# Two-layer diffusion backbone with top-2-of-8 experts: weights of the small experts split by halves, another order of products, and weighting, spreading and gather in other chunks

## Chip, cores and metric

One core of one Trainium2 chip runs the whole kernel in one launch. The metric is device time in microseconds (us), the median of several runs. The compute engines are named as in the profile: PE is the matrix engine (PEld its weight loads), DVE the vector engine, ACT the scalar engine, POOL the GpSimd engine, and SP issues the DMA transfers. Each engine works its instructions off in program order.

## The reference, cut to what matters

The layer stack is a short gated convolution with a dense feed-forward block (layer 0) and differential attention with a mixture of experts (layer 1). The change lies in the mixture of experts alone:

```python
def moe_ffn(a, w_r, b_r, w1, w3, w2):          # a: 256 tokens x 1024
    logits = (a @ w_r).astype(jnp.float32) + b_r.astype(jnp.float32)
    top_v, top_i = lax.top_k(logits, TOP_K)    # 2 of 8 experts for each token
    gates = jax.nn.softmax(top_v, axis=-1)
    ...
    # for each expert, on its tokens xs:
    #   (silu(xs @ w1) * (xs @ w3)) @ w2, times the gate, added back at the token
```

The feed-forward width is 2816, so an expert has 34.6 MB of weights in float32, and all eight together 277 MB.

## The kernel before, in words

**Two parts.** float32 values are split in two parts in a fast matrix format (F32R): a first part (`hi`, by a cast on ACT, L88) and the rest (`lo`, by a subtraction on DVE, L92). A product of split weights and split activations takes three matmuls (`mm3`, L200 to L202). The output stays close to a float32 product.

**Units.** Weights come in units of 128x2048 float32 (1 MB). `Loads` issues one DMA for each unit, in the order in which units are used, as soon as one of the raw slots (`rw`, `ra`, `rp`, `rq`) is free. `Parts` turns raw units into `hi`, `lo` in one of three slots: `Parts.unit()` gives the next unit to the caller, and before that it frees the slot of the unit used before and calls `pump`, which puts the cast and the subtraction of the next unit that isn't split yet into the queues of ACT and DVE. So the splits stand in the program where units are taken, about two units ahead of their use. `engines(u)` says in how many pieces a unit is split: two halves of 1024 columns for the units of the large experts, one piece of 2048 for those of the small experts.

**Experts.** The experts 2 to 7 are put in an order by their counts on the chip (`choose`). Places 2, 4 and 6 (`FEW`) hold at most 64 tokens, the others at most 128. For a small expert the two parts of its 64 tokens stand side by side as 128 columns, so a product needs two matmuls, by `hi` and by `lo` of the weights (`two`, L1237). Some units of the small experts (`whole`, the second unit of chunks 1, 4, 7 and 10) aren't split at all: they are used raw, with plain float32 matmuls (L1234).

**Chunks.** The hidden width is cut in 11 chunks. The main loop goes over the 88 pairs of expert and chunk, `g`. A chunk `c` of expert `e` does in this order: it takes its first unit and multiplies (`up`, first half of the 1024 inputs); it takes the unit of w2 of chunk `g-2` and multiplies (`finish`, `down`, into `y`); it turns the hidden values of chunk `g-1` (`hidden`: PE, then ACT and DVE in turn); it takes its second unit and multiplies (`up`, second half), and ACT copies or activates the result (`act`).

**Work between the experts.** Once the last `down` of an expert is done (two chunks into the next expert) `weighted` scales `y` by the gates and splits it (two ACT, two DVE instructions, from the one buffer of `y`), after the second of the four products of the second `up`. `spread` brings the result back to the tokens: eight matmuls in two PSUM tiles of the tag `g` (`psg`, two buffers) and four DVE instructions (L1308) that add to the stream. It is called twice, at the end of chunks 2 and 3. In an odd expert `gather` fetches the tokens of the next two experts in eight steps at the end of chunks 2 to 9: each step has four matmuls into a `psg` tile, an ACT or DVE instruction, two casts and, one step later, two subtractions. At the end a second loop over the experts serves only counts above the capacity; the trace has nothing of it.

Of the kernel before, what the change touches and what calls it, by code (L numbers as in the profile page):

```python
# [11 lines left out]
F32 = mybir.dt.float32  # L12
# [8 lines left out]
P = 128  # L21
D = 1024
KT = D // P
T = 256
T2 = 2 * T
# [11 lines left out]
FEW = (2, 4, 6)  # L37
# [105 lines left out]
def backbone(ctx: ExitStack, tc: tile.TileContext, i, out):  # L143
    nc = tc.nc
    V, A, PE, PO = nc.vector, nc.scalar, nc.tensor, nc.gpsimd
# [15 lines left out]
    units = [i["w0"][u] for u in range(49)] + [i["w1"][u] for u in range(16)]  # L161
    chosen, chunks = [], [(e, c) for e in range(NE) for c in range(NCH)]

    def moe_unit(e, u):

        if e < 2:
            return i["moe"][e, u]
        return lambda: i["moe"][bass.ds(chosen[e - 2], 1), u].rearrange("a p c -> (a p) c")


    whole, uses = [], []
    for g, (e, c) in enumerate(chunks):
        uses.append((e, 3 * c))
        if g > 1:
            uses.append((chunks[g - 2][0], 3 * chunks[g - 2][1] + 2))
        if e in FEW and c % 3 == 1:
            whole.append(len(units) + len(uses))
        uses.append((e, 3 * c + 1))
    uses += [(NE - 1, 3 * c + 2) for c in (NCH - 2, NCH - 1)]
    few = {len(units) + k for k, (e, _) in enumerate(uses) if e in FEW}  # L180
    units += [moe_unit(*u) for u in uses]
    ada_slots = raw_slots(const, 2, "ra")
    raws = raw_slots(const, 3, "rw")
# [3 lines left out]

    def engines(u):

        if u >= 69 and u not in few:  # L190
            return [(c, [(V, c)]) for c in (slice(0, 1024), slice(1024, U))]
        return [(ALL, [(V, ALL)])]

# [5 lines left out]
    def mm3(ps, wh, wl, xh, xl, first, last):  # L199
        PE.matmul(ps, wh, xh, start=first, stop=False)  # L200
        PE.matmul(ps, wh, xl, start=False, stop=False)  # L201
        PE.matmul(ps, wl, xh, start=False, stop=last)  # L202
# [149 lines left out]
    start = ExitStack()  # L352
# [8 lines left out]
    ps = [psc.tile([P, T2], F32, name=f"cb{n}") for n in range(4)]  # L361
# [48 lines left out]
    c = [sums(0)]  # L410
# [12 lines left out]
    run = ada_pe(1)  # L423
# [10 lines left out]
    def bank():  # L434
        return psp.tile([P, T2], F32, name="mm")
# [6 lines left out]
    w = parts  # L442
    first = [bank() for _ in range(6)]
# [16 lines left out]
    run = ada_pe(3)  # L460
# [30 lines left out]
    with tc.tile_pool(name="sc", bufs=1, reuse_waits="tile") as pc:  # L491
# [23 lines left out]
        for j in range(2, KT):  # L515
            ps = [bank() for _ in range(3)]
# [6 lines left out]
        ps = [bank() for _ in range(4)]  # L523
# [51 lines left out]
    with tc.tile_pool(name="ac", bufs=1, reuse_waits="tile") as pc, tc.tile_pool(name="ffn", bufs=9, reuse_waits="tile") as hp:  # L575
# [7 lines left out]
        def h_tile():  # L583
            return hp.tile([P, T2], F32R, name="hh"), hp.tile([P, T2], F32R, name="hl")
# [9 lines left out]
        h = [h_tile() for f in range(2)]  # L594
        ws = [[next(w) for k in range(2 * KT)] for f in range(2)]
        for s in range(2):
            for f in range(2):
                ps = [bank()[:, :T] for _ in range(2)]
# [8 lines left out]
        for gi, n in enumerate(GROUPS):  # L607
            while len(h) < n:
                ps = [bank() for _ in range(2)]
# [15 lines left out]
            for m in range(4 if lastg else KT):  # L625
                f = bank()
# [5 lines left out]
            h = []  # L632
# [64 lines left out]
    first = project(0, bank)  # L697
# [530 lines left out]
        V.tensor_copy(gs, ps)  # L1228
        return back, gs

    def two(ps, x, w, c, first, last):

        if w[1] is None:
            PE.matmul(ps, x.bitcast(F32), w[0][:, c], start=first, stop=last)  # L1234
        else:
            for b in range(2):
                PE.matmul(ps, x, w[b][:, c], start=first and b == 0, stop=last and b == 1)  # L1237

    def up(ps, xs, h, w, ks=range(4)):
        for k in ks:  # L1240
            c = slice(k * T2, (k + 1) * T2)
            a = h == k == 0, h == 1 and k == 3
            if len(xs) == 3:
                two(ps, xs[2][:, 4 * h + k], w, c, *a)
            else:
                mm3(ps, xs[0][:, 4 * h + k], xs[1][:, 4 * h + k], w[0][:, c], w[1][:, c], *a)

    def act(ps, few=False):
        if few:
# [8 lines left out]
    def hidden(g, few=False):  # L1258
        pt = pst.tile([P, T], F32, name="ht")
        if few:  # L1260
            for f in range(4):
                PE.matmul(pt[:, f * H:(f + 1) * H], g[:, f * P:(f + 1) * P], fold, start=True, stop=True)
            g = px.tile([P, P], F32, name="hg")
            A.activation(g, pt[:, :P], AF.Silu)
            V.tensor_tensor(out=g, in0=pt[:, P:], in1=g, op=OP.mult)
            hb = px.tile([P, T], F32R, name="hh").rearrange("p (f b s) -> p f b s", f=2, b=2)
            g = g.rearrange("p (f s) -> p f s", f=2)
            A.copy(hb[:, :, 0], g)
            V.tensor_tensor(out=hb[:, :, 1], in0=g, in1=hb[:, :, 0].bitcast(F32), op=OP.subtract)
            return [hb]  # L1270
        for f in range(2):
            PE.transpose(pt[:, f * P:(f + 1) * P], g[:, f * P:(f + 1) * P], ident)
        hh = px.tile([P, T], F32R, name="hh")
        hl = px.tile([P, T], F32R, name="hl")
        A.copy(hh, pt)  # L1275
        V.tensor_tensor(out=hl, in0=pt, in1=hh.bitcast(F32), op=OP.subtract)
        return hh, hl

    def down(y, h, w, first, last):
        for f, n in ((0, 0), (1, 0), (0, 1), (1, 1)):  # L1280
            b = slice(f * P, (f + 1) * P)
            c = slice(f * D + n * T2, f * D + (n + 1) * T2)
            a = first and f == 0, last and f == 1
            if len(h) == 1:
                two(y[n], h[0][:, f].rearrange("p b s -> p (b s)"), w, c, *a)
            else:
                mm3(y[n], h[0][:, b], h[1][:, b], w[0][:, c], w[1][:, c], *a)

    def weighted(y, g):

        yh, yl = ([px.tile([P, T2], F32R, name=f"{a}{n}") for n in range(2)] for a in ("yh", "yl"))
        for n in range(2):
            A.activation(yh[n], y[n], AF.Identity, scale=g)
        for n in range(2):
            V.scalar_tensor_tensor(yl[n], y[n], g, yh[n].bitcast(F32), op0=OP.mult, op1=OP.subtract)
        return list(zip(yh, yl))

    def spread(n, w, back):

        for k in range(4 * n, 4 * n + 4, 2):  # L1300
            ps = psg.tile([P, 2, T], F32, name="g")
            for j in range(2):
                c = slice((k + j) % 4 * P, ((k + j) % 4 + 1) * P)
                for b in range(2):
                    PE.matmul(ps[:, j], w[b][:, c], back, start=b == 0, stop=b == 1)
            for j in range(2):
                x = X[0][k + j]
                V.scalar_tensor_tensor(x, ps[:, j], mod1[20 + k // 2][:, j, 0:1], x, op0=OP.mult, op1=OP.add)  # L1308
# [14 lines left out]
    run, got, rets = gather(), {}, {}  # L1323
# [3 lines left out]
    res, parted, acts, hids, y = None, deque(), {}, {}, None  # L1327
# [10 lines left out]
    for g, (e, c) in enumerate(chunks):  # L1338
        n, pr, few_now = e % 2, e // 2, e in FEW
        ps = psh.tile([P, T2], F32, name="h13")  # L1340
        w = parts.unit()
        for k in range(4):
            if g == 0:
                next(run)
            up(ps, got[pr][n], 0, w, [k])
        if g == 0:
            next(run)
            for _ in range(2):
                parts.give(1)
            parts.holding = False  # L1350
        if g > 1:
            y = finish(g - 2)
            if chunks[g - 2][1] == NCH - 1:
                e0 = chunks[g - 2][0]
                res = y, rets[e0 // 2][1][:, e0 % 2:e0 % 2 + 1], rets[e0 // 2][0][:, e0 % 2]
        if g > 0:
            hids[g - 1] = hidden(acts.pop(g - 1), chunks[g - 1][0] in FEW)
        if g == 1:
            gates()
        if g == 2:  # L1360
            places_of()
            V.tensor_tensor(out=fold, in0=ident[:, :H], in1=ident[:, H:], op=OP.add)
        if g == 4:
            choose()
        w = parts.unit()
        for k in range(4):
            up(ps, got[pr][n], 1, w, [k])
            if k == 1 and res is not None:
                parted.extend((m, v, res[2]) for m, v in enumerate(weighted(*res[:2])))
                res = None  # L1370
        acts[g] = act(ps, few_now)
        if parted and c > 1:
            spread(*parted.popleft())
        if n == 0 and c == 4:
            rets[pr] = returns(pr)
        if n == 1 and e < NE - 1:
            if c == 1:
                for t in range(2):
                    onehot(t, pr + 1)
                run = gather(pr + 1)  # L1380
            if 2 <= c < 2 + KT:
                got[pr + 1] = next(run)
    y = finish(g - 1)
    hids[g] = hidden(acts.pop(g))
    y = finish(g)
    for n, w in enumerate(weighted(y, rets[3][1][:, 1:2])):
# [4 lines left out]
    _, count = nc.values_load_multi_w_load_instructions(r["cnti"][:1], min_val=0, max_val=T,  # L1391
                                                        skip_runtime_bounds_check_because="counts of 256 tokens")
    with tc.If(count[0] > 0):
        for e in range(NE):
            with tc.If(count[1 + e] > 0):
                n = e % 2
# [6 lines left out]
                y = acc()  # L1403
                for c in range(NCH):
                    w = []
# [7 lines left out]
                    ps = psh.tile([P, T2], F32, name="h13")  # L1413
# [88 lines left out]
```

## Time and profile before

| | us |
|---|---|
| median of 3 runs | 1651.02 (1650.89 to 1652.36) |
| the profiled execution | 1652.38 |
| its span, first to last instruction | 1650.7 |
| mixture of experts, first `up` to the end | 822.7 to 1650.7 |

The busy shares over the whole span are PE 94%, PEld 77%, DVE 78%, ACT 52%, POOL 3%; 400 MB come in by DMA at 243 GB/s on average. A matmul's record reaches to the end of its pipeline, so PE records overlap; the step from the start of one matmul to the next is what it costs. In a timeline a number in brackets is the time for which the engine sat idle ahead of the row, and what ended it.

### The profile page before, as it was taken

What the parts mean: (1) busy time and instruction counts of PE and PEld (TensorE: products, weight loads), DVE (VectorE), ACT (ScalarE), POOL (GpSimd) and SP (SyncE); (2) the same over time, 40 slices, a digit from 0 to 9 for tenths busy, and PEclk for the clock granted to TensorE, in tenths of its full rate; (3) what the DMA queues carried; (4) which work ended last, traced back from release to release, by engine and by line L of the source; (5) the groups of instructions that cost most, each with busy time, mean ns of one, the idle gap of its engine ahead of it and who ended that gap; (6) DMA issues with size and microseconds to landing.
All of it is one profiled execution on the core that took longest, in us unless ns stands there. A gap on an engine that the chain in (4) does not pass through costs nothing. (4 is left out here: it accounts for less than half of the span.)

```text
span 1650.7 us, 20590 instructions
## 1 busy us (share of the span) xinstructions
PE 1553.3 (94%) x7569; PEld 1264.6 (77%) x7569; DVE 1281.9 (78%) x1799; ACT 866.1 (52%) x1163; POOL 44.9 (3%) x162
## 2 busy tenths in 40 slices
PE   8799899999999999998899999888998889988997
PEld 7687688888888888887878778666786667866785
DVE  5888887668658666667588988878888788977896
ACT  3222244222212243445577768666676667866774
POOL 0000000000000002113000000000000000000000
PEclk9899999999999999999999999999999999999999
DMA  9345524445547424223469978889799997889990
GB/s 360 104 161 203 201 104 156 176 132 200 179 160 279 174 80 151 77 77 128 153 260 368 351 312 344 342 336 347 295 341 350 361 363 307 345 330 357 352 357 30
DMA packets 55727, 400.33 MB, mean 243 GB/s; under 512 B 6449, under 2 KB 6481, under 8 KB 7105
## 3 DMA queue, kind: packets, MB, share of 16 engines
q1 hardware_dynamic: 55298, 398.50, 64.4%
q8 instruction: 61, 1.00, 0.2%
q0 software_dynamic: 320, 0.44, 0.2%
q14 instruction: 48, 0.39, 0.1%
HBM read 397.87 MB, written 1.05 MB: 242 GB/s over the span
## 5 line engine op out<-in xcount | busy, mean ns | idle before, releaser
L92 DVE TENSOR_TENSOR wl<-rw,wh 128x1024 fp32r<-128x1024 f32 (+1 forms) x187 | 319.0, 1729 | 110.8 <-ACT wh L88 108.6
L88 ACT CAST wh<-rw 128x1024 fp32r<-128x1024 f32 (+1 forms) x186 | 264.8, 1453 | 63.3 <-PE mm L201 56.4
L200 PE MATMUL mm<-ah,wh 128*128 128x512 f32 (+1 forms) x576 | 221.5, 385 | 8.0 <-ACT ah L340 7.2
L202 PE MATMUL mm<-ah,wl 128*128 128x512 f32 (+1 forms) x576 | 221.1, 384 | 6.2 <-DVE wl L92 6.1
L201 PE MATMUL mm<-al,wh 128*128 128x512 f32 (+1 forms) x576 | 220.8, 383 | 0.0
L92 DVE TENSOR_TENSOR wl<-rp,wh 128x1024 fp32r<-128x1024 f32 (+1 forms) x122 | 174.9, 1465 | 35.0 <-ACT wh L88 31.4
L280 DVE SCALAR_TENSOR_TENSOR junk<-ra,cb 128x1024 bf16<-128x1024 f32 x136 | 166.3, 1223 | 3.3
L88 ACT CAST wh<-rp 128x1024 fp32r<-128x1024 f32 (+1 forms) x122 | 147.4, 1244 | 4.4 <-issue 1.7
L200 PE MATMUL h<-wh,xs 128*128 128x512 f32 x352 | 144.5, 410 | 0.0
L201 PE MATMUL h<-wl,xs 128*128 128x512 f32 x352 | 139.5, 396 | 0.0
L202 PE MATMUL h<-wh,xs 128*128 128x512 f32 x352 | 139.4, 396 | 0.0
L200 PEld LDWEIGHTS mm<-ah,wh 128*128 128x128 f32 x576 | 110.5, 192 | 30.2 <-ACT ah L340 8.5
L202 PEld LDWEIGHTS mm<-ah,wl 128*128 128x128 f32 x576 | 110.2, 191 | 28.9 <-DVE wl L92 8.4
L92 DVE TENSOR_TENSOR wl<-ra,wh 128x1024 fp32r<-128x1024 f32 (+1 forms) x81 | 114.5, 1444 | 20.2 <-ACT wh L88 19.4
L92 DVE TENSOR_TENSOR wl<-rq,wh 128x1024 fp32r<-128x1024 f32 (+1 forms) x87 | 124.3, 1476 | 6.8 <-ACT wh L88 6.4
L201 PEld LDWEIGHTS mm<-al,wh 128*128 128x128 f32 x576 | 110.3, 191 | 21.5 <-DVE al L335 0.9
L88 ACT CAST wh<-rq 128x1024 fp32r<-128x1024 f32 (+1 forms) x87 | 104.2, 1256 | 0.0
L88 ACT CAST wh<-ra 128x1024 fp32r<-128x1024 f32 (+1 forms) x81 | 96.7, 1230 | 2.7 <-PE h L202 2.0
L1237 PE MATMUL h<-wh,xl 128*128 128x512 f32 x216 | 89.9, 416 | 0.0
L1237 PE MATMUL h<-wl,xl 128*128 128x512 f32 x216 | 86.0, 398 | 2.3 <-DVE wl L92 2.3
L201 PE MATMUL y<-wl,hh 128*128 128x512 f32 x220 | 87.1, 396 | 1.1 <-DVE wl L92 1.1
L200 PE MATMUL y<-wh,hh 128*128 128x512 f32 x220 | 87.4, 397 | 0.5 <-ACT hh L1275 0.5
(328 smaller groups left out, 3057.1 us busy)
## 6 DMA issues: line engine op xcount, KB each, us to landing
rw<-moe SPq DMA_DIRECT2D x81, 1024.0 KB, 5.5
rp<-moe SPq DMA_DIRECT2D x77, 1024.0 KB, 5.7
rw<-w SPq DMA_DIRECT2D x61, 1024.0 KB, 4.9
rq<-moe SPq DMA_DIRECT2D x54, 1024.0 KB, 6.0
ra<-moe SPq DMA_DIRECT2D x52, 1024.0 KB, 5.7
ra<-ada SPq DMA_DIRECT2D x44, 1024.0 KB, 5.1
rx<-ada SPq DMA_DIRECT2D x4, 1024.0 KB, 19.7
rp<-w SPq DMA_DIRECT2D x4, 1024.0 KB, 6.6
```

The source lines that it names most:

```text
L88: self.nc.scalar.copy(hi[:, c0], raw[:, c0])
L92: engine.tensor_tensor(out=lo[:, c], in0=raw[:, c], in1=hi[:, c].bitcast(F32), op=OP.subtract)
L200: PE.matmul(ps, wh, xh, start=first, stop=False)
L201: PE.matmul(ps, wh, xl, start=False, stop=False)
L202: PE.matmul(ps, wl, xh, start=False, stop=last)
L280: V.scalar_tensor_tensor(junk, raw[:, a * D:(a + 1) * D], 1.0, cb[:, s], op0=OP.mult, op1=OP.mult, accum_out=m[:, a, s:s + 1])
L1237: PE.matmul(ps, x, w[b][:, c], start=first and b == 0, stop=last and b == 1)
```

## The change

The units of the small experts are split in two halves of 1024 columns, as those of the large experts are. The second unit of chunks 1, 3, 5, 7 and 9 is used whole, in place of 1, 4, 7 and 10. Products with first parts lead: for a small expert `few_up` issues two products with `hi` ahead of the two with `lo`, and `down` does the same for each half of its unit; for a large expert the product with the weights' `lo` comes third in place of second (`mm3w`), and `down` takes both outputs of the first half of its unit before the second half. In the loop `weighted` stands ahead of the second unit, and the first `spread` at the same place one chunk later, the second one at the end of that chunk: both are in chunk 2. `gather` runs in chunks 3 to 10. Other lines are as they were; the number of DMA transfers is the same.

```diff
-        if e in FEW and c % 3 == 1:
+        if e in FEW and c % 2:
             whole.append(len(units) + len(uses))
...
-        if u >= 69 and u not in few:
+        if u >= 69:
             return [(c, [(V, c)]) for c in (slice(0, 1024), slice(1024, U))]
         return [(ALL, [(V, ALL)])]
...
+    def few_up(ps, x, w, h, ks):
+
+        for b in range(2 if w[1] is not None else 1):
+            for k in ks:
+                v = x[:, 4 * h + k]
+                PE.matmul(ps, v.bitcast(F32) if w[1] is None else v, w[b][:, k * T2:(k + 1) * T2], start=h == k == b == 0,
+                          stop=h == 1 and k == 3 and (b == 1 or w[1] is None))
+
+    def mm3w(ps, xh, xl, wh, wl, first, last):
+        PE.matmul(ps, xh, wh, start=first, stop=False)
+        PE.matmul(ps, xl, wh, start=False, stop=False)
+        PE.matmul(ps, xh, wl, start=False, stop=last)
...
     def down(y, h, w, first, last):
-        for f, n in ((0, 0), (1, 0), (0, 1), (1, 1)):
...
+        for f in range(2):
+            cs = [slice(f * D + n * T2, f * D + (n + 1) * T2) for n in range(2)]
             if len(h) == 1:
-                two(y[n], h[0][:, f].rearrange("p b s -> p (b s)"), w, c, *a)
+                for b in range(2):
+                    for n in range(2):
+                        PE.matmul(y[n], h[0][:, f].rearrange("p b s -> p (b s)"), w[b][:, cs[n]], start=first and f == b == 0,
+                                  stop=last and f == b == 1)
             else:
-                mm3(y[n], h[0][:, b], h[1][:, b], w[0][:, c], w[1][:, c], *a)
+                for n in range(2):
+                    mm3w(y[n], h[0][:, f * P:(f + 1) * P], h[1][:, f * P:(f + 1) * P], w[0][:, cs[n]], w[1][:, cs[n]],
+                         first and f == 0, last and f == 1)
...
         if g > 0:
             hids[g - 1] = hidden(acts.pop(g - 1), chunks[g - 1][0] in FEW)
+        if res is not None:
+            parted.extend((m, v, res[2]) for m, v in enumerate(weighted(*res[:2])))
+            res = None
+        elif parted:
+            spread(*parted.popleft())
...
         w = parts.unit()
-        for k in range(4):
-            up(ps, got[pr][n], 1, w, [k])
-            if k == 1 and res is not None:
-                parted.extend((m, v, res[2]) for m, v in enumerate(weighted(*res[:2])))
-                res = None
+        for k in range(0, 4, 2):
+            up(ps, got[pr][n], 1, w, [k, k + 1])
         acts[g] = act(ps, few_now)
         if parted and c > 1:
             spread(*parted.popleft())
...
-            if 2 <= c < 2 + KT:
+            if 3 <= c < 3 + KT:
                 got[pr + 1] = next(run)
```

## Rows read from the trace of the kernel before

**Rows 1.** Page, part 1: busy us, share of the span, instructions.

```profile
PE 1553.3 (94%) x7569; PEld 1264.6 (77%) x7569; DVE 1281.9 (78%) x1799; ACT 866.1 (52%) x1163; POOL 44.9 (3%) x162
```

**Rows 2.** Windows, experts 2, 4, 5, 6: us; PE, PEld, DVE, ACT, POOL; PEclk, DMA, GB/s.

```profile
1025.00:1126.90 101.90, 89.58 (x384) 66.02 (x382) 78.07 (x67) 67.66 (x68) 0.00 (x0) 0.95 0.90 343
1232.90:1330.60 97.70, 86.40 (x384) 63.94 (x382) 76.98 (x66) 66.38 (x67) 0.00 (x0) 0.98 0.93 354
1330.60:1435.20 104.60, 100.34 (x467) 81.59 (x466) 92.15 (x119) 77.43 (x109) 0.00 (x0) 1.00 0.86 335
1435.20:1535.70 100.50, 88.14 (x382) 65.25 (x381) 77.84 (x67) 67.56 (x68) 0.00 (x0) 0.97 0.90 346
```

**Rows 3.** Waits of DVE in expert 6 (1435.2 to 1535.7): us in total, times, longest.

```profile
DVE wl L92 <- ACT wh L88: 18.3, 14, 2.2
DVE hh L1269 <- ACT hh L1268: 3.6, 10, 0.4
```

**Rows 4.** Waits of PE in expert 6, the same stretch.

```profile
PE y L1237 <- DVE wl L92: 9.3, 6, 1.8
PE y L1237 <- DVE yl L1295: 1.7, 1, 1.7
```

**Rows 5.** Timeline of DVE and ACT, expert 4, around one wait: start, us, what.

```profile
1284.61 0.28 DVE L1265 TENSOR_TENSOR hg<-ht,hg 128x128 f32<-128x128 f32 x1
1287.07 2.29 DVE L92 TENSOR_TENSOR wl<-ra,wh 128x2048 fp32r<-128x2048 f32 x1 [1.52 <-ACT wh L88]
...
1284.93 0.30 ACT L1268 CAST hh<-hg 128x128 fp32r<-128x128 f32 x1 [1.30 <-DVE hg L1265]
1285.13 1.90 ACT L88 CAST wh<-ra 128x2048 fp32r<-128x2048 f32 x1
```

**Rows 6.** Timeline of PE in and behind the same wait.

```profile
1289.41 0.50 PE L1237 MATMUL y<-wl,hh 128*128 128x512 f32 x1 [1.82 <-DVE wl L92]
1289.75 0.40 PE L1237 MATMUL y<-wh,hh 128*128 128x512 f32 x1
1289.98 0.50 PE L1237 MATMUL y<-wl,hh 128*128 128x512 f32 x1
...
1290.71 0.63 PE L1237 MATMUL y<-wl,hh 128*128 128x512 f32 x1
1291.13 0.63 PE L1237 MATMUL y<-wh,hh 128*128 128x512 f32 x1
```

**Rows 7.** Timeline of PE's weight loads while a whole unit is multiplied.

```profile
1302.39 0.19 PEld L1234 LDWEIGHTS h<-rp,xl 128*128 128x128 f32 x1 [0.24 <-issue]
1302.82 0.19 PEld L1234 LDWEIGHTS h<-rp,xl 128*128 128x128 f32 x1 [0.24 <-issue]
```

**Rows 8.** A unit split by halves (timeline, expert 7); L92 by itself: min/median/max ns.

```profile
1594.95 2.00 ACT L88 CAST wh<-rp 128x1024 fp32r<-128x1024 f32 x2
1596.04 2.36 DVE L92 TENSOR_TENSOR wl<-rp,wh 128x1024 fp32r<-128x1024 f32 x2 [0.52 <-ACT wh L88]
...
L92 DVE TENSOR_TENSOR wl<-rw,wh x125: 1208/1219/2294, 806.5 to 1631.5; 128x1024 fp32r<-128x1024 f32 x98, 128x2048 fp32r<-128x2048 f32 x27
```

**Rows 9.** Windows, expert 5: chunks 2 and 3; then chunks 5 and 6.

```profile
1347.00:1372.10 25.10, 20.84 (x102) 16.82 (x101) 23.37 (x34) 14.42 (x21) 0.00 (x0) 1.00 0.83 320
1381.20:1399.30 18.10, 18.10 (x85) 14.79 (x85) 16.28 (x22) 14.29 (x22) 0.00 (x0) 1.00 0.90 346
```

**Rows 10.** Timeline of DVE and PE in chunks 1 and 2 of expert 5.

```profile
1349.13 1.40 DVE L1295 SCALAR_TENSOR_TENSOR yl<-y,gs,yh 128x512 fp32r<-128x512 f32 x2
1359.05 1.65 DVE L1308 SCALAR_TENSOR_TENSOR xl<-g,mod,xl 128x256 f32<-128x256 f32 x4
...
1359.97 0.39 PE L1197 MATMUL g<-oh,nh 128*128 128x256 f32 x1 [3.01 <-DVE xl L1308]
```

**Rows 11.** Windows: ten us of expert 4; chunks 6 and 7 of expert 7.

```profile
1250.00:1260.00 10.00, 8.36 (x45) 6.76 (x43) 7.61 (x7) 7.05 (x8) 0.00 (x0) 1.00 1.01 406
1588.70:1605.90 17.20, 17.20 (x78) 13.95 (x77) 15.53 (x17) 12.86 (x16) 0.00 (x0) 1.00 0.98 371
```

More of the change, by code (lines that the diff above doesn't have):

```diff
@@ L179, in backbone @@
     uses += [(NE - 1, 3 * c + 2) for c in (NCH - 2, NCH - 1)]
-    few = {len(units) + k for k, (e, _) in enumerate(uses) if e in FEW}
     units += [moe_unit(*u) for u in uses]
@@ L1229, in returns @@
         return back, gs
[L1231 to L1237, printed above, removed]
+    def few_up(ps, x, w, h, ks):
[8 more added lines that the diff above has]
+        PE.matmul(ps, xh, wl, start=False, stop=last)
     def up(ps, xs, h, w, ks=range(4)):
+        if len(xs) == 3:
+            few_up(ps, xs[2], w, h, ks)
+            return
         for k in ks:
             c = slice(k * T2, (k + 1) * T2)
[L1242 to L1246, printed above, removed]
+            mm3w(ps, xs[0][:, 4 * h + k], xs[1][:, 4 * h + k], w[0][:, c], w[1][:, c], h == k == 0, h == 1 and k == 3)
     def act(ps, few=False):
@@ L1279, in down @@
     def down(y, h, w, first, last):
-        for f, n in ((0, 0), (1, 0), (0, 1), (1, 1)):
-            b = slice(f * P, (f + 1) * P)
-            c = slice(f * D + n * T2, f * D + (n + 1) * T2)
-            a = first and f == 0, last and f == 1
+        for f in range(2):
+            cs = [slice(f * D + n * T2, f * D + (n + 1) * T2) for n in range(2)]
             if len(h) == 1:
-                two(y[n], h[0][:, f].rearrange("p b s -> p (b s)"), w, c, *a)
-            else:
-                mm3(y[n], h[0][:, b], h[1][:, b], w[0][:, c], w[1][:, c], *a)
+                for b in range(2):
+                    for n in range(2):
+                        PE.matmul(y[n], h[0][:, f].rearrange("p b s -> p (b s)"), w[b][:, cs[n]], start=first and f == b == 0,
+                                  stop=last and f == b == 1)
+            else:
+                for n in range(2):
+                    mm3w(y[n], h[0][:, f * P:(f + 1) * P], h[1][:, f * P:(f + 1) * P], w[0][:, cs[n]], w[1][:, cs[n]],
+                         first and f == 0, last and f == 1)
     def weighted(y, g):
@@ L1341, in backbone @@
         w = parts.unit()
-        for k in range(4):
+        for k in range(0, 4, 2):
             if g == 0:
-                next(run)
-            up(ps, got[pr][n], 0, w, [k])
+                for _ in range(2):
+                    next(run)
+            up(ps, got[pr][n], 0, w, [k, k + 1])
         if g == 0:
@@ L1365, in backbone @@
         w = parts.unit()
-        for k in range(4):
-            up(ps, got[pr][n], 1, w, [k])
-            if k == 1 and res is not None:
-                parted.extend((m, v, res[2]) for m, v in enumerate(weighted(*res[:2])))
-                res = None
+        for k in range(0, 4, 2):
+            up(ps, got[pr][n], 1, w, [k, k + 1])
         acts[g] = act(ps, few_now)
```

## The prediction

> **What bounds the kernel now.** I read the page's busy shares first: PE 94%, DVE 78% [rows 1]. These are averages, so the next view is the windows, cut at the experts' first product. The change touches nothing before the mixture of experts, so only these stretches count. A large expert in its steady chunks has PE busy all the time: two chunks take 18.1 us with the gather and 17.2 us without it, and DVE is busy for 16.28 and 15.53 of them [rows 9, 11]. There PE is the bound, with DVE close behind. A small expert is another matter: it takes 97.7 to 101.9 us, PE is busy 86 to 90 of them, and the granted clock falls to 0.95 to 0.98 [rows 2]; DVE is busy for 77 to 78, so it idles for 20 to 24 us.
>
> The waits say how the two hang together. In expert 6 PE waits 9.3 us, six times, for subtractions in `down`, and once 1.7 us for `yl` [rows 4]. DVE in turn waits 18.3 us, 14 times, for ACT's casts, and 3.6 us for the small cast inside `hidden` [rows 3]. The timeline of one wait shows the chain: DVE does `hg`, ACT casts `hh` and only then starts the cast of the next unit at 1285.13, for 1.90 us; DVE sits idle 1.52 us and subtracts from 1287.07 for 2.29 us [rows 5]; PE has begun `down` of that unit and waits 1.82 us until 1289.41 [rows 6]. So a small expert is bound by a chain that goes around ACT and DVE: whole casts, whole subtractions, and the hidden values' turns between them. [...]
>
> In the large experts time is lost in chunks 2 and 3: 25.1 us in expert 5 where two steady ones take 18.1 [rows 9]. PE waits 3.01 us for a `psg` tile that the gather wants while DVE has yet to read the spread results out of it (1359.05, 1.65 us) [rows 10].
>
> **Part 1: halves and first parts, small experts.** The units split whole are 29 per expert (33 less 4), after the change 28 by halves. DVE starts its subtraction 1.94 us after ACT's cast starts when it is whole (1285.13 to 1287.07) [rows 5] and 1.09 us after when it is halved (1594.95 to 1596.04), and its wait is 0.52 us in place of 1.52 behind a similar turn of the hidden values [rows 8]. So the rows show that DVE is released by the first half alone, and a wait of 1.5 us becomes one of 0.5. Of the 14 waits I take 11 as full ones: 11 us off the chain per expert. Against it stands the price of the second instruction: a halved pair takes 2.36 us on DVE and 2.00 on ACT, the whole one 2.29 and 1.90 [rows 5, 8]; 28 x 0.07 = 2.0 us more on DVE, and one unit less takes away 2.3. That is nothing within 0.5 us. DVE's view of a small expert: 100 us (mean of three [rows 2]) - 11 = 89.
>
> Seen from PE: the first half of the unit is ready 0.85 us sooner by ACT and 2.29 - 1.2 = 1.1 us sooner by DVE, some 1.9 us, and with two `hi` products ahead PE asks for `lo` 0.23 us later. A wait of 1.82 [rows 6] just vanishes; the second half follows 1.2 us behind the first, while PE needs four products (0.93 us) for a half, so 0.2 us may be left. Taking away 9.3 + 1.7 us of waits from expert 6 [rows 4], and half of the 6 us that a mean clock of 0.97 over 100 us means at the lower level [rows 2], leaves 100.5 - 11.0 - 3.0 = 86.5.
>
> The whole units cost PE more: a weight load every 0.43 us, eight for a unit [rows 7], against eight products at 0.23: 3.4 against 1.9 us. One more such unit per expert is +1.6 us of PE, and PE's view gives 88. It buys a better spacing: with every second chunk whole, PE's long chunk always stands beside three splits and its short one beside two, where before two short ones followed each other. The two views give 88 and 89. I take 89, -11 us for each of the three, **-33 us**; ends: 84 us (DVE's remaining waits hidden as well, -48 in all) and 96 us (waits that only move, -12).
>
> [...]
>
> **Part 2: weighting, spreading, gather.** `weighted` is two ACT instructions and two on DVE (1.40 us [rows 10]). It moves ahead of a unit's cast and subtraction and of two products. `y` has one buffer, so PE's first `down` of the new expert, a chunk later, waits for it: the 1.7 us of rows 4, once per small expert. With 2.3 us of splitting behind it rather than ahead, that wait goes; it is in the 11.0 above. What is now behind it, the split of one unit, comes 1.4 us later; it has a chunk's time until it is used, so I cost that at nothing. Without this cover it would be 1.4 us per expert.
>
> The first `spread` (eight matmuls, four DVE instructions of 1.65 us together [rows 10]) goes from the end of chunk 2 to its middle, past one unit's split and the second `up`; the second from the end of chunk 3 to that of chunk 2, past three splits. A wait is new: the second spread needs both `psg` tiles back while DVE may not have read them. Between the two PE has only an `up` (1.9 us small, 2.8 large). Queueing up DVE's work of expert 5 by hand (weighting, then four one-hot instructions, two splits, `hl`, the four reads) the reads end about 58.4 where PE arrives at 56.8: about 1.5 us, with chunk 3's first `up` queued behind it on PE. The gather step that waited 3.01 us there is gone from chunk 2, and in chunk 3 the tiles have long been read. By that queue chunks 2 and 3 take 21.0 us in place of 25.1: -4.1. For three such experts that is 12 us. DVE carries the same sum of work, though, and in chunks 4 to 10 it is within a tenth of PE [rows 9], so part comes back as short waits: I take **-7 us**, ends 0 and -13. Expert 7 gathers nothing, so it pays the new wait without the gain; that is in the -7. The gather's last step, now in chunk 10, is (18.1 - 17.2)/2 = 0.45 us of PE moved, not added [rows 9, 11]; its reader is the second `up` of the next expert, past one `up` and one `down`.
>
> **Part 3: what costs nothing.** `mm3w` and the order in `down` keep the number of matmuls and ask for `lo` one product later; where PE never waits that gives no time, hidden or not. Grouped gather steps in the first chunk: within 1 us. SP issues the same transfers; a whole unit keeps its raw slot until PE is through, one more per small expert. Ten microseconds of expert 4 carried 406 GB/s [rows 11], where the forecast needs 34.6 MB in 89 us, 389 GB/s. So the cover is there, and thin.
>
> **Sum.** 1652.4 (the profiled execution: 1650.7 span and 1.7 around it) - 33 - 7 = 1612.4; this execution lies 1.4 above the median, so 1611.
>
> **Rivals.** *Transfers take over.* For it: in chunks 6 and 7 of expert 7 the DMA share is 0.98 at only 371 GB/s [rows 11], and the small experts already run at 0.90 to 0.93 [rows 2]. Against: 406 GB/s for ten us. At 371 a small expert takes 34.6 MB / 371 = 93.3 us, -6.7 each: -20 - 7, 1624. *Waits only move.* The hidden turns themselves (`hg`, `hh`) hold ACT in order, so the next cast starts as late as before and the next unit is the late one. Then only the `yl` wait (3 x 1.7) and the 7 us go, and the whole units cost 4.8: 1644. The same time would come if PE had to wait for the second half anyhow. Against it: the 0.52 us wait in rows 8. *All waits go.* Small experts at 84, large ones at the lower end: -48 - 13, 1590. *Slower: the second spread blocks.* Place: end of chunk 2 of the seven experts 1 to 7, PE in order behind `psg`. Price: the wait there times seven, with chunk 3's products, and all casts that wait for their slots, behind it. The gains of 40 us are gone when it reaches 1.5 + 40 / 7 = 7.2 us. That needs both splits of the chunk (4.7 us) to stand ahead of the reads beside the 1.5 us that I counted, 6.2, and the slow clock behind it, 1.7 us more (3 us in expert 6 for two such falls, roughly). At 7.9 us it is 1611 + 7 x 6.4 = 1656. The nearest row is 3.01 us [rows 10].
>
> **How the numbers follow.** A difference of 0.2% (3.3 us) is about what can be told from none. Chances: forecast 0.60 (1598 to 1626 by the ends of its terms), transfers 0.14, waits move 0.13 (0.05 of it within 0.2%), all waits go 0.06, second spread blocks 0.07. Faster 0.60 + 0.14 + 0.08 + 0.06 = 0.88, same 0.05, slower 0.07. The range goes from 1594, inside the case where all goes, to 1641, inside the one where waits move: it leaves out about 0.2.
>
> **What would show it.** In the windows of experts 2, 4 and 6: 87 to 91 us each, a granted clock of 0.98 or more, DVE's waits for ACT about 0.5 us each and under 9 us in all. In the waits of PE: `y` for `wl` below 3 us per expert, `yl` gone, and a new row, the spread matmul for `xl`, near 1.5 us per expert. Chunks 2 and 3 of expert 5 near 21 us. Wrong would be: DVE waiting for DMA, or PE for `back` products for over 3 us, or small experts above 95 us.

## The result and the profile after

The changed kernel takes 1592.38 us (median of 4 runs, 1590.91 to 1594.94) against 1650.95 for the kernel before: a ratio of 0.9645, 95% interval 0.9629 to 0.9662, or 58.6 us less. The forecast was 1611, with a range from 1594 to 1641: the measured time lies 1.6 us below the range. The sign and the places of the gain were right, the size was not.

Windows of the changed kernel's trace, cut at the first product of experts 2, 4, 5 and 6, and the last one at chunks 2 and 3 of expert 5 (us; PE, PEld, DVE, ACT, POOL busy; granted clock, DMA share, GB/s):

```profile
1022.10:1106.10 84.00, 83.95 (x384) 63.56 (x383) 74.60 (x92) 64.79 (x93) 0.00 (x0) 1.00 0.99 390
1207.50:1291.50 84.00, 83.95 (x385) 63.55 (x384) 74.58 (x92) 64.75 (x93) 0.00 (x0) 1.00 0.99 390
1291.50:1392.90 101.40, 99.95 (x466) 81.25 (x465) 93.56 (x121) 78.92 (x111) 0.00 (x0) 1.00 0.93 363
1392.90:1476.80 83.90, 83.85 (x383) 63.50 (x383) 74.48 (x92) 64.65 (x93) 0.00 (x0) 1.00 0.98 387
1307.50:1329.30 21.80, 20.35 (x98) 16.16 (x97) 21.80 (x33) 14.94 (x19) 0.00 (x0) 1.00 0.91 354
```

Beside [rows 2]: a small expert takes 84.0 us in place of 97.7 to 101.9, PE is busy through all of it, and the granted clock is 1.00 in all three. Expert 5 takes 101.4 in place of 104.6, its chunks 2 and 3 21.8 in place of 25.1 [rows 9]. Summed over the experts of the two traces: small ones -48.2 us, experts 1, 3 and 5 -11.9, expert 0 -1.0, expert 7 +1.1, and the whole stage to the end of the trace -60.5. Ahead of the stage, in lines that the change leaves as they are, the trace of the changed kernel is 2.1 us longer (first `up` at 824.8 against 822.7).

Waits of DVE in expert 6 of the changed kernel, then those of PE in the whole expert stage up to the last chunk (us in total, times, longest):

```profile
DVE wl L92 <- ACT wh L88: 5.2, 9, 0.7
DVE hh L1272 <- ACT hh L1271: 3.7, 10, 0.4
...
PE g L1312 <- DVE xl L1315: 3.3, 3, 1.4
PE h L1241 <- DVE wl L92: 1.6, 1, 1.6
PE y L1241 <- DVE wl L92: 0.5, 1, 0.5
PE h L1239 <- ACT wh L88: 0.2, 1, 0.2
```

DVE's 18.3 us [rows 3] have become 5.2, at most 0.7 each, and PE's waits for `wl` and `yl` in the small experts [rows 4] are gone; the three other rows lie ahead of expert 2. The one new wait is the forecast one: the second spreading waits for `psg`. DVE's and PE's timeline in chunk 2 of expert 5:

```profile
1317.93 1.65 DVE L1315 SCALAR_TENSOR_TENSOR xl<-g,mod,xl 128x256 f32<-128x256 f32 x4
...
1322.10 1.65 DVE L1315 SCALAR_TENSOR_TENSOR xl<-g,mod,xl 128x256 f32<-128x256 f32 x4
...
1318.85 0.38 PE L1312 MATMUL g<-back,yh 128*128 128x256 f32 x1 [1.37 <-DVE xl L1315]
```

### The profile page after: what moved, and what is told of

It reads as the page before. It is cut to its first block, busy times and chain, and to the rows that moved or that the text cites. A ratio compares the mean times of both kernels' runs of the same rounds, so it can differ in the third digit from the quotient of the medians.

```text
span 1592.3 us, 20866 instructions
## 1 busy us (share of the span) xinstructions
PE 1540.4 (97%) x7569; PEld 1259.1 (79%) x7569; DVE 1278.5 (80%) x1880; ACT 864.8 (54%) x1244; POOL 44.7 (3%) x162
## 5 line engine op out<-in xcount | busy, mean ns | idle before, releaser
L92 DVE TENSOR_TENSOR wl<-rw,wh 128x1024 fp32r<-128x1024 f32 (+1 forms) x208 | 315.9, 1548 | 86.4 <-ACT wh L88 85.8
L92 DVE TENSOR_TENSOR wl<-rp,wh 128x1024 fp32r<-128x1024 f32 (+1 forms) x152 | 183.3, 1246 | 17.9 <-ACT wh L88 17.2
L88 ACT CAST wh<-rp 128x1024 fp32r<-128x1024 f32 (+1 forms) x152 | 155.4, 1070 | 2.6 <-PE h L1240 2.4
L1239 PE MATMUL h<-wh,xs 128*128 128x512 f32 x352 | 142.4, 404 | 0.0
L92 DVE TENSOR_TENSOR wl<-rq,wh 128x1024 fp32r<-128x1024 f32 x102 | 119.5, 1219 | 9.9 <-ACT wh L88 9.4
L92 DVE TENSOR_TENSOR wl<-ra,wh 128x1024 fp32r<-128x1024 f32 x96 | 113.0, 1218 | 6.7 <-ACT wh L88 6.1
L88 ACT CAST wh<-rq 128x1024 fp32r<-128x1024 f32 x102 | 101.2, 1048 | 2.1 <-PE h L1240 2.1
L88 ACT CAST wh<-ra 128x1024 fp32r<-128x1024 f32 x96 | 95.9, 1048 | 0.0
L1239 PE MATMUL y<-wh,hh 128*128 128x512 f32 x220 | 87.1, 396 | 0.5 <-ACT hh L1278 0.5
L1240 PE MATMUL y<-wh,hl 128*128 128x512 f32 x220 | 86.9, 395 | 0.0
L199 PE MATMUL mm<-wh,ah 128*128 128x256 f32 (+1 forms) x256 | 83.7, 327 | 0.0
```

What stands on the lines that cost most here:

```text
L88: self.nc.scalar.copy(hi[:, c0], raw[:, c0])
L92: engine.tensor_tensor(out=lo[:, c], in0=raw[:, c], in1=hi[:, c].bitcast(F32), op=OP.subtract)
L1239: PE.matmul(ps, xh, wh, start=first, stop=False)
L1240: PE.matmul(ps, xl, wh, start=False, stop=False)
```

## The experiments

Two theories stood against each other. H: the halves carry the gain of the small experts. S: the even spacing of the whole units carries it, because it evens DVE's load. Then there are the places of weighting, spreading and gather, and the order of products. Each part was undone in the changed kernel (u) and, save the order, done alone in the kernel before (a). Expert times are from first product to first product in each run's trace; us by ratio is (ratio - 1) x 1651.

| kernel | median us | ratio, 95% interval | us by ratio | experts 2, 4, 6 | experts 1, 3, 5 |
|---|---|---|---|---|---|
| before | 1650.95 | 1 | 0 | 101.8, 97.7, 100.6 | 104.3, 106.0, 104.6 |
| changed | 1592.38 | 0.9645 (0.9629 to 0.9662) | -58.6 | 84.0, 84.0, 84.0 | 100.3, 101.4, 101.4 |
| u1 whole splits | 1616.69 | 0.9784 (0.9763 to 0.9806) | -35.7 | 90.3, 91.9, 91.9 | 100.3, 102.6, 102.6 |
| u2 third whole | 1599.47 | 0.9688 (0.9671 to 0.9706) | -51.5 | 87.8, 87.8, 87.8 | 100.4, 100.0, 100.0 |
| u3 old order | 1592.74 | 0.9645 (0.9628 to 0.9662) | -58.6 | 84.6, 84.5, 84.5 | 100.4, 100.8, 100.8 |
| u4 old places | 1610.20 | 0.9752 (0.9736 to 0.9769) | -40.9 | 84.9, 85.0, 85.0 | 104.3, 108.0, 106.9 |
| a1 halves alone | 1622.31 | 0.9818 (0.9789 to 0.9847) | -30.0 | 90.7, 90.7, 90.7 | 105.8, 103.8, 103.7 |
| a2 spacing alone | 1641.46 | 0.9932 (0.9911 to 0.9952) | -11.2 | 94.6, 93.1, 94.7 | 104.3, 107.4, 107.6 |
| a4 places alone | 1641.46 | 0.9932 (0.9910 to 0.9953) | -11.2 | 99.0, 97.4, 100.1 | 100.3, 100.8, 100.8 |
| n0 none whole | 1625.45 | 0.9847 (0.9831 to 0.9863) | -25.3 | 93.4, 93.4, 93.4 | 100.3, 103.3, 103.3 |
| q4 quarters | 1594.53 | 0.9654 (0.9637 to 0.9670) | -57.1 | 84.4, 84.4, 84.4 | 100.3, 101.7, 101.7 |
| b1 spread in 2 and 3 | 1587.29 | 0.9607 (0.9580 to 0.9633) | -64.9 | 83.6, 83.6, 83.6 | 100.3, 100.4, 100.4 |
| b2 four whole | 1592.94 | 0.9643 (0.9627 to 0.9659) | -58.9 | 85.7, 85.7, 85.7 | 100.3, 100.3, 100.3 |

**u1, halves undone.**

```diff
-        if u >= 69:
+        if u >= 69 and u not in few:
```

> The changed kernel, with one part undone: the small experts' units are split in one piece of 2048 columns again. Theory H (the halves carry the gain: DVE starts 0.85 us sooner behind each cast and PE behind the first half): the chain over ACT and DVE binds again. For two chunks DVE needs 5 x 2.29 + 2 x 0.57 for the hidden values + 2 x 0.36 + 2 x 1.5 us of waits = 16.3 us against PE's 14.5, so a small expert takes 90 to 95 us in place of 84, and the kernel 1610 to 1625. Theory S (the even spacing of the whole units carries it, halves are extra): PE's 14.5 us per two chunks still bind, small experts stay under 86 us and the kernel under 1599.

23 us of the 58.6 go back and the small experts stand at 90.3 to 91.9: H's time, and S alone is out. Waits of PE in experts 2 to 6 of u1:

```profile
PE y L1290 <- DVE wl L92: 14.1, 13, 1.6
PE g L1313 <- DVE xl L1316: 4.4, 5, 1.4
```

**u2, spacing undone.**

```diff
-        if e in FEW and c % 2:
+        if e in FEW and c % 3 == 1:
```

> The changed kernel, but the second units of chunks 1, 4, 7 and 10 are used whole, as before, in place of 1, 3, 5, 7 and 9. Theory H (halves): PE has 1.6 us less to do for each small expert and still binds, 82.5 us each, kernel 1587 to 1589. Theory S (spacing): three chunks hold eight splits, on DVE 8 x 2.36 + 3 x 0.57 + 3 x 0.36 + waits of 0.6 us = 23.5 us, against PE's 6.9 + 6.9 + 7.65 = 21.4, so PE waits 2 us in each three chunks, 88 to 90 us for a small expert, kernel 1604 to 1612.

H alone is out too: with 1.6 us less to do for PE, a small expert takes 3.8 us more. S's rate was nearly met (87.8 against 88 to 90), so both parts are needed. The kernel's 1599.5 us lies between the two forecasts, because experts 3, 5 and 7 take 1.0 to 1.4 us less than in the changed kernel. Between 1000 and 1500 us PE waits in 18 places that the changed kernel doesn't have:

```profile
PE y L1289 <- ACT wh L88: 5.1, 9, 0.8
PE y L1289 <- DVE wl L92: 4.8, 9, 0.5
```

**u3, the old order of products** (`two` and `mm3` for `few_up` and `mm3w`, `down` by outputs).

> The changed kernel with the order of products of before (hi and lo in turn, and in down by outputs, not by halves). By the trace of the changed kernel, in which PE doesn't wait for subtractions in the small experts, DVE is ahead by more than the 0.2 to 0.7 us that the new order gives: kernel 1592 to 1594, and small experts 84 us. If the order carries a part of the gain, PE waits for wl reappear in the small experts, 0.2 to 1 us in each chunk, up to 33 x 0.5 = 16 us: 1600 to 1610.

No difference in the whole time. Chunks 7 and 9 of the small experts take 0.23 to 0.35 us more (7.98 to 8.00 and 7.88 to 7.89 against 7.65 us), and some chunks take less; the order is worth about 0.5 us for each small expert, which the large ones give back.

**u4, the old places.**

```diff
-        if res is not None:
-            parted.extend(...)
-            res = None
-        elif parted:
-            spread(*parted.popleft())
...
             up(ps, got[pr][n], 1, w, [k, k + 1])
+            if k == 0 and res is not None:
+                parted.extend(...)
+                res = None
...
-            if 3 <= c < 3 + KT:
+            if 2 <= c < 2 + KT:
```

> The changed kernel with weighting, spreading and gather at their old places. Experts 1, 3 and 5 lose what they gained (4.0, 4.7 and 3.2 us), expert 7 stays, and PE's wait for yl comes back in the small experts (1.7 us each, perhaps with the slower clock behind it): 1592 + 12 + 5 = 1609; 1604 if the halves hide the wait for yl.

The time was met (1610.2 against 1609), but by luck, since neither term was: experts 1, 3 and 5 lose 4.0, 6.6 and 5.5 us, 16.1 where 12 were forecast, and the small ones 0.9 to 1.0 each, 2.9 where 5 were. Chunks 2 and 3 of expert 3 take 28.9 us, more than the 26.6 of the kernel before. Experts 3, 5 and 7 have a wait for `yl` of 1.1 us each (the row of `L1239`) that the kernel before doesn't have there, and the granted clock is 0.97 and 0.98 in experts 3 and 5, where it was 0.98 and 1.00. In the small experts the wait for `yl` is 0.4 us each, in two parts: the halves hide most of it (a1 has 0.3 each, a2 1.7), and the 1.7 us of [rows 4] were no term of their own. Waits of PE in u4's expert stage:

```profile
PE g L1196 <- DVE xl L1315: 12.0, 6, 3.0
PE y L1239 <- DVE yl L1302: 3.3, 3, 1.1
...
PE y L1289 <- DVE yl L1302: 1.3, 6, 0.3
```

**a1, a2, a4: one part alone in the kernel before.** The edits are those of u1, u2 and u4 the other way round.

> The kernel before with one part of the change: the small experts' units split by halves. By the prediction's DVE view 11 waits of 1.5 us become 0.5: small experts from 100 to 89 us, kernel 1651 - 33 = 1618 (1614 to 1626). If halves help only together with the spacing (eight splits in three chunks keep DVE the bound), 94 to 97 us each and 1633 to 1642.

> The kernel before with one part of the change: the second units of chunks 1, 3, 5, 7 and 9 whole. The prediction charged this with +1.6 us of PE for each small expert, 1656. If it evens DVE's load, as the undone halves showed with all else changed (90 to 92 us for a small expert), small experts come to 92 to 94 us: 1651 - 3 x 7 = 1630 (1626 to 1634).

> The kernel before with one part of the change: weighting, spreading and gather at the new places. The prediction's terms: 7 us in the large experts and 1.7 us for yl in each small one, 1639. From the trace of the changed kernel: 4.0 + 4.7 + 3.2 in experts 1, 3 and 5, +0.5 in expert 7, 5 for yl: 1634. Undoing it in the changed kernel cost 18 us; if it is worth as much alone, 1633; if less, it matters more when small experts run at PE's pace.

Halves alone bring 30 us, with small experts at 90.7: the forecast's DVE view (89) almost to the point. Spacing alone brings 11 us where the prediction charged 4.8 and the text ahead of the run forecast 21. It takes 93 to 95 us for a small expert, but experts 3 and 5 lose 1.4 and 3.0 us by it: u4 shows the same. That DVE enters the next expert's crowded chunks less far ahead when the small expert was fast would explain it; the waits for `yl` in experts 3 and 5 fit (0.4 us each in a2, 1.1 in u4, none before), but it isn't measured by itself. Places alone bring 11 us where 12 to 18 were forecast. In the trace, which is of the fastest of a4's five runs (1634.79 us), experts 1, 3 and 5 take 13.0 us less and the small ones 3.6: the wait for `yl` is gone from these, and the longer ones for `wl` stay. So the three sum to 52 us alone and do 59 together. Halves and spacing simply add (u4 holds both and the order: 41, alone 30 + 11). The 6 us on top go with the places, worth 11 us in the slow kernel and 18 in the fast one; with intervals of some 3 us on each of these figures, the size of this surplus is loose.

**n0, no whole unit** (`c % 2` becomes `c > NCH`), to measure DVE's pace by itself.

> The changed kernel without whole units: all 33 units of a small expert are split by halves. PE has 5 x 1.6 = 8 us less to do (76 us), so DVE must bind, and the time shows what a chunk costs on DVE. Busy time alone: 3 x 2.29 + 2 x 0.29 = 7.45 us, 82 us for 11 chunks and 5 for weighting and spreading: 87. The prediction's chain (with 0.36 and 0.7 us of waits in each chunk): 8.5 us, 94 + 5 = 99. Kernel 1601 by the first, 1630 to 1637 by the second.

Steady chunks with three splits take 8.51 to 8.54 us: the chain of the forecast (8.5), not the busy time. DVE's timeline over one such chunk:

```profile
1481.85 0.29 DVE L1272 TENSOR_TENSOR hh<-hg,hh 128x128 fp32r<-128x128 f32 x1 [0.36 <-ACT hh L1271]
1482.79 2.36 DVE L92 TENSOR_TENSOR wl<-rq,wh 128x1024 fp32r<-128x1024 f32 x2 [0.65 <-ACT wh L88]
1485.17 2.36 DVE L92 TENSOR_TENSOR wl<-rw,wh 128x1024 fp32r<-128x1024 f32 x2
1487.45 2.35 DVE L92 TENSOR_TENSOR wl<-rp,wh 128x1024 fp32r<-128x1024 f32 x2
1489.72 0.28 DVE L1268 TENSOR_TENSOR hg<-ht,hg 128x128 f32<-128x128 f32 x1
1490.37 0.29 DVE L1272 TENSOR_TENSOR hh<-hg,hh 128x128 fp32r<-128x128 f32 x1 [0.36 <-ACT hh L1271]
```

From `hh` to `hh` it is 8.52 us: three splits at 2.27 to 2.38, two small instructions, and two waits of 0.36 and 0.65 that no whole unit takes away. The whole expert takes 93.4, not 99: chunks 0 and 1 (6.73 and 7.43 us) run on the lead that DVE brings along. So the kernel's 1625.5 us lies between the two forecasts.

**q4, four pieces of 512 columns.**

> The changed kernel with the small experts' units split in four pieces of 512 columns. DVE idles 9.5 us in each small expert of the changed kernel. If an instruction more costs what single ones cost (144 ns), 56 of them are 8 us on DVE and 10 or so on ACT: small experts 84 to 88 us, kernel 1592 to 1604. If back to back they cost 0.03 to 0.07 us, the idle time takes it: 84 us, 1592.

84.4 us: 56 more instructions on DVE cost 0.4 us of a small expert. Rows of DVE, two units back to back:

```profile
1451.57 2.50 DVE L92 TENSOR_TENSOR wl<-rw,wh 128x512 fp32r<-128x512 f32 x4
1453.98 2.49 DVE L92 TENSOR_TENSOR wl<-rp,wh 128x512 fp32r<-128x512 f32 x4
```

A unit takes 2.41 us from start to start here, 2.28 in halves and 2.21 to 2.27 whole: 0.06 us for each further instruction.

**b1, the second spreading in the middle of chunk 3.**

```diff
-        if parted and c > 1:
-            spread(*parted.popleft())
```

> The changed kernel, but the second spreading stands in the middle of chunk 3 in place of the end of chunk 2. PE's wait for the psg tiles (1.4 us in experts 3 and 5, 0.6 in expert 7) then falls away, since DVE has a chunk's time to read them. If the wait is the loss: -1.4 x 2 - 0.6 = -3.4 us, 1589. If DVE's sum of work in chunks 1 to 3 is the loss, PE waits elsewhere for as long: 1592.

1587.3 us by median, 5 us under the changed kernel and below both; the intervals of the two ratios just overlap (0.9633 and 0.9629). In the traces the stretch from the first product to the end is 763.5 against 767.5 us. Of PE's waits for `psg` tiles between 1000 and 1500 us one row is left, the gather's in experts 3 and 5:

```profile
PE g L1196 <- DVE xl L1315: 1.1, 2, 0.6
```

Chunks 2 and 3 take 1.0 us less in experts 3 and 5 and 1.3 less in expert 7. The loss was the wait for `psg`, then, not the sum of DVE's work.

**b2, b1 with chunk 1's second unit split.**

> The changed kernel with the second spreading in the middle of chunk 3 (which took 5 us off), and the second unit of chunk 1 split in place of whole. If PE's products alone set the small experts' 83.6 us, each gets 1.6 us shorter: 1587 - 5 = 1582. If DVE is full in chunks 0 to 2, where it also has the weighting and the spreading, PE waits there instead: 1587 or up to 3 us above.

PE gets 1.6 us less to do and each small expert takes 2.1 us more; the kernel is 5.7 us slower than b1, beyond even the slower forecast. PE waits there, in the chunks with weighting and spreading:

```profile
PE y L1289 <- DVE wl L92: 5.6, 6, 1.4
PE y L1289 <- ACT wh L88: 1.4, 3, 0.5
```

So in the changed kernel PE and DVE are matched closely: one split more, in chunk 1, makes PE wait, and five more (n0) cost 9.4 us per small expert.

## Why the prediction was wrong, point by point

**What bounds, right.** The chain around ACT and DVE, with the 1.5 us wait for a whole cast, was what held the small experts: halving it alone gave 30 us, and the wait became 0.65 where the forecast took 0.5 from [rows 8]. DVE's timeline of the changed kernel in chunk 7 of expert 6 and into chunk 8 shows three splits, the turn of the hidden values, and the next two:

```profile
1448.10 2.36 DVE L92 TENSOR_TENSOR wl<-rq,wh 128x1024 fp32r<-128x1024 f32 x2 [0.66 <-ACT wh L88]
1450.49 2.36 DVE L92 TENSOR_TENSOR wl<-rw,wh 128x1024 fp32r<-128x1024 f32 x2
1452.77 2.35 DVE L92 TENSOR_TENSOR wl<-rp,wh 128x1024 fp32r<-128x1024 f32 x2
1455.04 0.28 DVE L1268 TENSOR_TENSOR hg<-ht,hg 128x128 f32<-128x128 f32 x1
1455.68 0.29 DVE L1272 TENSOR_TENSOR hh<-hg,hh 128x128 fp32r<-128x128 f32 x1 [0.36 <-ACT hh L1271]
1456.63 4.75 DVE L92 TENSOR_TENSOR wl<-rw,wh 128x1024 fp32r<-128x1024 f32 x4 [0.66 <-ACT wh L88]
```

**The term that failed: -11 us per small expert, measured -16 (48.2 for three).** The measured 84 is the term's own lower end. The step that failed is the choice of 89 from the two views, DVE's 89 and PE's 88, and each view has a fault. First, DVE's: the spacing was entered as a cost of 1.6 us of PE, and its effect ("a better spacing") got no number. By n0's measure DVE needs 8.5 us for a chunk of three splits and 8.5 - 2.3 = 6.2 for one of two. Two chunks of the changed kernel make 14.7 on DVE (14.79 in the rows above, from `hh` to `hh`) against PE's 7.65 + 6.89 = 14.5: even to 0.2 or 0.3 us, which DVE's lead carries. Three chunks of the old spacing make 8.5 + 8.5 + 6.2 = 23.2 against PE's 6.5 + 6.5 + 8.1 = 21.1 (steps of 0.23, and 1.6 more for the whole unit): DVE binds, and u2 took 22.2 and 23.3 us for chunks 5 to 7 and 8 to 10. That sum was to be had from the rows: 3 x 2.36 + 0.52 + 0.36 + 2 x 0.28 = 8.5 [rows 3, 5, 8]. The forecast took 11 us off the mean of three experts and so kept the old spacing's bound, which is what a1 measured: 90.7. With the new spacing (and the order, which gives nothing) on top of a1, u4 measures 84.9.

Second, PE's own view was 88 and not 84, since the waits were counted too short. The row of 1.82 us [rows 6] is idle time behind the end of the matmul before, and that end is that of its pipeline:

```profile
1287.09 0.50 PE L1237 MATMUL y<-wh,hh 128*128 128x512 f32 x1
```

From this start to the next at 1289.41 it is 2.32 us, where a step is 0.23: 2.09 us were lost, 0.27 more than the row says. And two rows of PE's waits in expert 6, beside those of [rows 4], weren't entered:

```profile
PE h L1237 <- DVE wl L92: 0.7, 1, 0.7
PE y L1237 <- ACT wh L88: 0.6, 2, 0.3
```

By the steps the ten waits of expert 6 lost 14.6 us, where the rows of idle time say 12.3 and the forecast entered 11.0: 3.6 of the 4 us. The 3.0 us for the clock in the same view are the author's estimate from the mean of 0.97 over 100 us [rows 2], with a lower level of half the full clock; no run shows them as a time of their own. What the trace of the kernel before shows in expert 6 is two falls: a granted clock of 0.54 from 1474.2 to 1477.2 us and 0.89 in the 3 us after it, 0.64 from 1528.2 to 1531.2 and 0.79 after it, and 1.00 in the other stretches of 3 us.

**-7 us in the large experts, measured -11.9 in experts 1, 3 and 5, or -10.8 with expert 7, which the -7 includes.** The queue worked out by hand was good: 1.5 us of new wait forecast, 1.37 found; -4.1 forecast for chunks 2 and 3 of expert 5, -3.3 found, and -12.5 for experts 1, 3 and 5 together where 12 were said. The step that failed is the discount: "part comes back as short waits" in chunks 4 to 10. Nothing came back; chunks 4 to 9 take 9.04 to 9.10 us as before, and chunk 10 the 0.44 to 0.48 us more of the gather's step that moved there. And by u4 the places are worth 18 us once the small experts are fast, so they are no term apart from the others.

**What cost nothing, right.** The order of products gave nothing measurable by u3, and the whole unit costs PE what was said: 14.54 us for a pair of chunks against 2 x 6.48 in u2's chunks without a whole unit and without a wait, 1.58 us.

**Rivals.** Transfers didn't take over: the small experts drew 387 to 390 GB/s at a DMA share of 0.98 to 0.99, and no wait for a transfer stands among PE's or DVE's in the expert stage (the kernel before has 1.5 and 3.0 us of them on DVE in experts 2 and 4). An expert's 34.6 MB in 84 us would be 412 GB/s; the rest came in ahead: experts 3 and 5 drew 361 and 363 GB/s for 101.4 us each, 36.6 and 36.8 MB. Waits that only move, and the blocking second spreading, are out by the tables of waits. The rival in which all waits go (1590) is what happened; it was given 0.06, since DVE's 89 was taken as what binds, and the range was closed at 1594, above the 1590 to which the lower ends of its own two terms add. It was to be weighed against DVE's view once the load of two chunks was summed on each engine.

**The fixed cost of an instruction.** A further instruction has one price by itself and another back to back. From subtractions by themselves a further one costs 0.144 us (1219 and 2294 ns [rows 8]: twice the first less the second), and a 512-column one gives about the same: 685 ns (median in q4), and 2 x 685 - 1219 = 151 ns. Back to back, the row that the forecast went by gives 0.07 (2.36 less 2.29 [rows 5, 8]). By q4 the price of each further one back to back is 0.06 us: the row's price was the right one.

## What to carry to other kernels

Where two engines share a pipeline of few slots, sum their work over the period of the schedule (here two or three chunks) and not over the whole expert: spacing the chunks that are long on one engine evenly among those that are long on the other was worth 7 to 11 us beside the halves' 23 to 30, though it added work to the busiest engine. Cut an operation in pieces where the next engine in a chain waits for the whole of it; the wait shrank from 1.5 to 0.65 us for 0.06 us a piece. A wait in a list of PE is read by the step from start to start, not by the idle time alone.

## What the runs showed of the hardware that was not expected

Transfers kept up at 390 GB/s for 84 us on end with a DMA share of 0.99, and neither PE nor DVE waited for them. With no PE wait in the small experts the granted clock was 1.00 in experts 2, 4 and 6, where it had been 0.95 to 0.98 [rows 2]. But not behind every wait was it lower: in expert 4 of the kernel before it was 0.52 from 1290 to 1293 us, behind the wait of 1.82 us at 1289.41, with steps of 0.42 us in place of 0.23 [rows 6], and 1.00 from 1269 to 1286, where a wait of the same length ended at 1271.19.
